# Reordering the down projection of a hybrid decoder layer: pair order, late sums, five low parts by an adding DMA, and Silu one step later

## The chip, the cores and the metric

The kernel runs on one core of one Trainium2 chip. TensorE (PE) multiplies matrices, VectorE (DVE) and ScalarE (ACT) work element by element, GpSimd (POOL) is used little, and SyncE (SP) issues most of the DMAs. Each engine takes its instructions in program order. The metric is the device time of one execution in microseconds (us).

## The reference

One layer on 256 tokens of width 1024, in float32. A normalized input goes through `w_in` into two groups: eight heads of attention (with 256 tokens there is one block, so it is plain causal attention, after QK-norm and rotary), and a gated causal depthwise convolution with layer norm and Silu. Both go through `w_out` and are added to the input. Then comes the feed-forward part, with 2816 inner columns, which the change touches:

```
h = rms_norm(x, norm2_g[l])
x = x + (jax.nn.silu(h @ w_gate[l]) * (h @ w_up[l])) @ w_down[l]
```

## The kernel before, in words

**High and low parts.** To keep float32 accuracy every weight is split into a high part (rounded, type float32r, tile `wh`) and a low part (weight minus high part, tile `wl`). A product is then three matmuls: high by high, low by high and high by low. Weights come from HBM in blocks of 128x2048 (`raw`, a ring of 4, loaded by `load_block` on SP's queue), and are split in pieces of 128x1024, numbered from 0 on. `feed(upto)` converts high parts up to piece `upto + 1` on ACT (L243) and makes low parts up to piece `upto`: on DVE (L207), or, for some pieces, "by DMA": ACT writes the negative of the high part into `wl` (L204) and a DMA on POOL's queue adds the raw piece to it (L205). `wh` and `wl` are rings of 7, so piece j waits until PE has done with piece j-7. A block is reloaded when both its pieces are split.

**Stages.** Pieces 0 to 19 are `w_in`, 20 to 27 `w_out`, 28 to 71 gate and up (each f of 22 has two pieces: eight k tiles of gate and eight of up, for 128 inner columns), from 72 on `w_down`.

**Steps.** The order of the work is written out as steps. `step()` lets each task that is due issue its next part; a task is a generator that yields how many steps it waits. In gate and up there are four steps to an f; `feed` stands ahead of a step and runs 4 pieces ahead of PE (`LEAD`). When an f has reached the middle, its `glu_task` starts: one step later the gate is evicted (`halves`: ACT copies one half of the bank, L273, DVE adds it to the other half, L274), DVE multiplies by the row factor (L786) and ACT takes Silu (L788). Two steps after that the up bank is evicted in the same way and multiplied (L800).

**Plain and Strassen pairs.** The down projection goes over 11 pairs of 256 inner columns. A pair marked P is plain: two pieces, 24 matmuls of 512 columns. A pair marked F is done by a form of Strassen's algorithm with seven products instead of eight (M1, M2, N3, N4, N5, M6, M7, of 3 matmuls each): three pieces, the first of which is a raw quarter pair, the others weight sums made by three DVE adds (`add_up`, L221 to L223), and one extra quarter, `b11`, split apart by `single` (L190 and L191, for product M1). The other operand is sums of activations, `forms` (L810 to L819). All pairs add into the same eight banks of PSUM: M1, N5, M7 and M6 take, in this order, the ring `mm`, which held the gates of f=18 to 21; M2 and N3 take ring `t`; N4 and C22 take ring `s`, which held the ups of f=20 and 21. The last two Strassen pairs end the kernel product by product (`ends`), so that the final sums on DVE and the output DMAs can follow.

`SUMS` tells at which piece of gate and up `add_up` is called ahead of time for the first Strassen pairs; the others are made when the first of their pieces is converted.

Of the kernel before, what the change touches and what calls it, by code (L numbers as in the profile page):

```python
# [21 lines left out]
W = 512  # L22
# [3 lines left out]
NF = FF // P  # L26
# [30 lines left out]
V_PIECE = 21  # L57
SS_WAIT = 3
OUT_LATE = 6
PAIRS = "FPFPFPFPPFF"  # L60
FAST = [p for p in range(NF // 2) if PAIRS[p] == "F"]
PLAIN = [p for p in range(NF // 2) if PAIRS[p] == "P"]
DOWN = 72
DMA_LOW = 40
X_TOK = 12
SUMS = {66: 0, 70: 1}


def _round12(a):
# [59 lines left out]
def build(nc, tc, t):  # L129
    with ExitStack() as ctx:  # L130
        _build(nc, tc, t, ctx)
    keep_order(nc, tc)


def _build(nc, tc, t, ctx):
# [32 lines left out]
    def step():  # L168
        for task in list(tasks):
            while task in tasks and task[0] <= now[0]:  # L170
                try:
                    task[0] = now[0] + next(task[1])
                except StopIteration:
                    tasks.remove(task)
        now[0] += 1
# [4 lines left out]
    def load_block(i, parts=1):  # L180
        if i >= NB:
            return
        r = raw.tile([P, BW], F32, name=f"raw{i}", tag="raw")
        n = BW // parts
        for j in range(parts):
            nc.sync.dma_start(r[:, j * n:(j + 1) * n], t["w"][i - 2][:, j * n:(j + 1) * n])
        blocks[i] = r
# [5 lines left out]
    def new_piece():  # L193
        j = len(pieces)
        pieces.append([wgt.tile([P, PIECE], F32R, name=f"w{s}{j}", tag="w" + s) for s in "hl"])
        i, a = divmod(j * PIECE, BW)
        if j >= DOWN:
            return pieces[-1], down_piece(*down[j - DOWN]), j
        return pieces[-1], blocks[i][:, a:a + PIECE] if i > 1 else None, j

    def low_part(dst, src, by_dma=False):

        if by_dma:
            nc.scalar.activation(dst[1], dst[0].bitcast(F32), AF.Copy, scale=-1.0)  # L204
            nc.gpsimd.dma_start(dst[1].bitcast(F32), src, accum_op=ALU.add)  # L205
        else:
            nc.vector.tensor_tensor(dst[1], src, dst[0].bitcast(F32), op=ALU.subtract)  # L207
# [6 lines left out]
    wsums, b11 = {}, {}  # L214

    def add_up(q):

        if q not in wsums:
            w = blocks[DOWN // 2 + FAST[q]]
            u = wsums[q] = keep.tile([P, 4 * W], F32, name=f"t{q}", tag=("x2T", "big_l")[q % 2])  # L220
            nc.vector.tensor_tensor(u[:, 0:2 * W], w[:, 0:2 * W], w[:, W:3 * W], op=ALU.add)  # L221
            nc.vector.tensor_tensor(u[:, 2 * W:3 * W], u[:, 0:W], w[:, 2 * W:3 * W], op=ALU.add)
            nc.vector.tensor_tensor(u[:, 3 * W:], u[:, 2 * W:3 * W], w[:, 3 * W:], op=ALU.add)  # L223

    def down_piece(p, a):
        w = blocks[DOWN // 2 + p]
        if p in PLAIN:
            return w[:, a * PIECE:(a + 1) * PIECE]
        add_up(FAST.index(p))
        u = wsums[FAST.index(p)]  # L230
        return (w[:, 2 * W:], u[:, 0:2 * W], u[:, 2 * W:])[a]

    def single(q):

        i = DOWN // 2 + FAST[q]
        split(b11[q % 2], blocks[i][:, 0:W], nc.vector)
        load_block(i + RAW)

    def feed(upto):
        last = DOWN + len(down) - 1  # L240
        while len(pieces) <= min(upto + 1, last):
            dst, src, j = new_piece()
            nc.scalar.activation(dst[0], src, AF.Copy)  # L243
            waiting.append((dst, src, j))
        while waiting and waiting[0][2] <= upto:
            dst, src, j = waiting.pop(0)
            low_part(dst, src, DMA_LOW <= j < DOWN and j % 4 == 1)
            if j < DOWN and j % 2:
                load_block(j // 2 + RAW)
            elif j >= DOWN and down[j - DOWN][0] in PLAIN and down[j - DOWN][1]:  # L250
                load_block(DOWN // 2 + down[j - DOWN][0] + RAW)

    def wtile(col, width):
        j, c = divmod(col, PIECE)
        return [p[:, c:c + width] for p in pieces[j]]
# [15 lines left out]
    def halves(out, bank, side):  # L271

        nc.scalar.activation(side, bank[:, T:], AF.Copy)  # L273
        nc.vector.tensor_tensor(out, bank[:, 0:T], side, op=ALU.add)  # L274
# [79 lines left out]
    for kt in range(KT):  # L354
        if kt % 2 == 0:
            dst, _, _ = new_piece()
# [315 lines left out]
    for chunk in range(5):  # L672
        banks = [mm_bank(f"p{chunk}{i}") for i in range(NT)]
        for kt in range(KT):
# [3 lines left out]
            w = wtile(unit * W, W)  # L678
# [104 lines left out]
    def glu_task(f, pg, pu):  # L783
        tg = late.tile([P, T], F32, name=f"tg{f}", tag="tg", bufs=2)
        halves(tg, pg, side(f"gs{f}"))
        nc.vector.tensor_tensor(tg, tg, r_bc, op=ALU.mult)  # L786
        s = late.tile([P, T], F32, name=f"sf{f}", tag="sf", bufs=2)
        nc.scalar.activation(s, tg, AF.Silu)  # L788
        yield max(1, ffn["up"][f] - now[0])
        pair, second = divmod(f, 2)  # L790
        if pair in PLAIN:
            ac = late.tile([P, T], F32, name=f"ac{f}", tag="ac")
        else:
            q = FAST.index(pair)
            if not second:
                pair_sums[q] = late.tile([P, 9 * P], F32, name=f"ps{q}", tag="ps")
            ps = pair_sums[q]
            ac = ps[:, 0:T] if second else ps[:, T:2 * T]
        halves(ac, pu, side(f"us{f}"))
        nc.vector.tensor_tensor(ac, ac, s, op=ALU.mult)  # L800
        if pair in PLAIN:
            a = 2 * PLAIN.index(pair) + second
            nc.scalar.activation(acts[:, 0, a, :], ac, AF.Copy)
            yield 1
            nc.vector.tensor_tensor(acts[:, 1, a, :], ac, acts[:, 0, a, :].bitcast(F32), op=ALU.subtract)
        elif second:


            p3 = ps.rearrange("p (b q) -> p b q", q=P)
            nc.vector.tensor_tensor(p3[:, 4:6], p3[:, 2:4], p3[:, 0:2], op=ALU.subtract)  # L810
            nc.vector.tensor_tensor(p3[:, 6:8], p3[:, 5:6].to_broadcast([P, 2, P]), p3[:, 2:5:2], op=ALU.subtract)
            nc.vector.tensor_tensor(p3[:, 8], p3[:, 2], p3[:, 3], op=ALU.subtract)
            yield 1
            parts = ((forms[q][:, :, 0:3], p3[:, 0:3]), (forms[q][:, :, 3:7], p3[:, 5:9]))
            for to, of in parts:
                nc.scalar.activation(to[:, 0], of, AF.Copy)
            yield 1
            for to, of in parts:
                nc.vector.tensor_tensor(to[:, 1], of, to[:, 0].bitcast(F32), op=ALU.subtract)  # L819
# [16 lines left out]
    for f in range(NF):  # L836
# [6 lines left out]
        a = 0  # L843
        for g, group in enumerate(groups):
            jobs = []
            for z, k in group:
                if a % 4 == 0:
                    if f == a == 0:
                        step()
                    now_at = (off + a * P) // PIECE  # L850
                    if now_at in SUMS and a % 8 == 4:
                        add_up(SUMS[now_at])
                    feed(now_at + LEAD)
# [10 lines left out]
        if f == 0:  # L864
            spawn(glu_task(0, pg, pu), GLU0_WAIT)
            ffn["up"][0] = now[0] + GLU0_WAIT
# [9 lines left out]
    M1, M2, N3, N4, N5, M6, M7, C22 = range(8)  # L876
# [11 lines left out]
    def plain(pair, a):  # L888
        f = 2 * PLAIN.index(pair) + a
        w = pieces[index[pair, a]]  # L890
        for n in range(2):
            step()
            wn = [p[:, n * W:(n + 1) * W] for p in w]
            for l, r in ((0, 0), (1, 0), (0, 1)):
                for i in range(NT):
                    add((M2, N3, N4, C22)[2 * i + n], acts[:, l, f, i * P:(i + 1) * P], wn[r],
                        i == n == r == a == 1 and pair == PLAIN[-1])
# [4 lines left out]
    def seventh(q, m):  # L902
        form, part, side = of[m]
        rhs = b11[q % 2] if part is None else [p[:, side * W:(side + 1) * W] for p in pieces[index[FAST[q], part]]]
        for l, r in ((0, 0), (1, 0), (0, 1)):
            add(m, forms[q][:, l, form, :], rhs[r], r == 1 and q == len(FAST) - 1)

    ends = range(len(FAST) - 2, len(FAST))
    for pair in range(NF // 2 - 2):
        for q in range(1, len(FAST)):  # L910
            if min(FAST[q], FAST[-2]) == pair + 1:
                single(q)
        if pair in PLAIN:
            for a in range(2):
                feed(index[pair, a] + LEAD)
                plain(pair, a)
        else:
            q = FAST.index(pair)
            for part, ms in ((0, (M1, M2, N3)), (1, (N5, M7)), (2, (M6, N4))):
                feed(index[pair, part] + LEAD)  # L920
                step()
                for m in ms:
                    seventh(q, m)
# [12 lines left out]
    m1, u = rest[:, 0, :], rest[:, 1, :]  # L936
# [77 lines left out]
```

## Time and profile before

| | us |
|---|---|
| median of 3 runs | 297.55 (297.11 to 298.29) |
| profiled execution | 300.1 |
| its span, first to last instruction | 298.3 |
| PE busy | 289.8 |
| DVE busy | 245.7 |
| ACT busy | 188.9 |
| POOL busy | 28.2 |

The page shows one execution. It divides the span into 40 slices of 7.46 us and gives each engine's busy share in tenths, and the TensorE clock that was granted (PEclk, 9 for full). A row of the timeline holds the start, the duration, the engine, the line of the kernel, the operation, the tiles (output, then inputs), how many instructions are merged, and in brackets how long the engine had been idle and what released it. A row of the windows holds a stretch of time, its length, and the busy time of each engine in it.

### The profile page before, as it was taken

To read this page: it belongs to the slowest core of one execution; us is meant where nothing else is said; L and a number is where in the kernel's file an instruction comes from. 1 tells how busy PE (TensorE), PEld (TensorE's weight loads), DVE (VectorE), ACT (ScalarE), POOL (GpSimd) and SP (SyncE) were. 2 spreads that over 40 slices of the span, in tenths; PEclk is the share of its full clock that TensorE was granted. 3 is DMA by queue.
4 is the path that set the end of the run, shared out by engine and by line. 5 is a ranking of instruction groups with operands and counts; after the bars stand their busy time and mean duration, and the time that the engine had idled before them with its cause. 6 is when DMAs were issued, how large, how long until landed. Compare 5 with 4: busy or idle time off the path is not lost.

```text
span 298.3 us, 4308 instructions
## 1 busy us (share of the span) xinstructions
PE 289.8 (97%) x1567; PEld 244.6 (82%) x1567; DVE 245.7 (82%) x442; ACT 188.9 (63%) x320; POOL 28.2 (9%) x49
## 2 busy tenths in 40 slices
PE   8999999999999999999999999999999699999994
PEld 6778877678799988898888888888888478888883
DVE  3889995998996998874886785885688899999965
ACT  4777768977638883557767757756645486567400
POOL 0005372000000350001011001101010000000000
PEclk9999999999999999999999999999999959999999
DMA  7999779534313827353767768768756333760003
GB/s 249 418 414 357 301 249 332 193 141 161 123 23 137 341 79 288 124 169 129 226 182 301 233 179 311 249 158 310 262 125 271 141 143 142 281 266 18 0 0 141
DMA packets 11479, 60.92 MB, mean 204 GB/s; under 512 B 1537, under 2 KB 2145, under 8 KB 5570
## 3 DMA queue, kind: packets, MB, share of 16 engines
q1 hardware_dynamic: 9874, 55.14, 49.0%
q0 software_dynamic: 1440, 5.50, 8.6%
q8 instruction: 12, 0.20, 0.3%
q14 instruction: 9, 0.07, 0.1%
q10 hardware_dynamic: 144, 0.00, 0.0%
HBM read 55.40 MB, written 1.05 MB: 189 GB/s over the span
## 4 chain that ended last, share of the span: by engine, by line
PE 73%; DVE 14%; ACT 6%; issue 3%; DMA 2%; DVEq 0%; SPq 0%; ACTq 0%
PE p L685 18%; PE sum L886 16%; PE fg L264 10%; PE fu L264 10%; PE fg L269 5%; PE fu L269 5%; DVE wl L207 4%; ACT wh L243 3%; DMA first<-first 2%; PE po L285 2%; DVE x L932 2%; PE S L519 1%; PE pT L549 1%; DVE g L728 1%; DVE x2T L753 1%
## 5 line engine op out<-in xcount | busy, mean ns | idle before, releaser
L207 DVE TENSOR_TENSOR wl<-raw,wh 128x1024 fp32r<-128x1024 f32 x76 | 92.6, 1233 | 0.3 <-ACT wh L243 0.3
L243 ACT ACTIVATE wh<-raw 128x1024 fp32r<-128x1024 f32 x84 | 86.8, 1048 | 7.6 <-PE sum L886 4.8
L264 PE MATMUL fg<-g,wh 128*128 128x512 f32 x176 | 44.9, 394 | 0.3 <-DVE g L728 0.3
L264 PE MATMUL fu<-g,wh 128*128 128x512 f32 x176 | 44.6, 394 | 0.0
L264 PEld LDWEIGHTS fg<-g,wh 128*128 128x128 f32 x176 | 31.6, 189 | 6.3 <-DVE g L728 0.7
L264 PEld LDWEIGHTS fu<-g,wh 128*128 128x128 f32 x176 | 31.7, 189 | 5.7
L685 PE MATMUL p<-wh,xh 128*128 128x512 f32 x80 | 33.1, 414 | 0.1
L788 ACT ACTIVATE sf<-tg 128x256 f32<-128x256 f32 x22 | 9.2, 418 | 36.7 <-DVE tg L786 36.7
L685 PE MATMUL p<-wh,xl 128*128 128x512 f32 x80 | 31.4, 392 | 0.0
L886 PE MATMUL sum<-wh,forms 128*128 128x512 f32 x72 | 23.2, 405 | 2.7 <-DVE tg L274 2.7
L269 PEld LDWEIGHTS fg<-g,wl 128*128 128x128 f32 x176 | 24.1, 190 | 1.8
L269 PEld LDWEIGHTS fu<-g,wl 128*128 128x128 f32 x176 | 24.1, 190 | 1.7
L685 PE MATMUL p<-wl,xh 128*128 128x512 f32 x80 | 25.2, 395 | 0.0
L269 PE MATMUL fu<-g,wl 128*128 128x256 f32 x176 | 24.8, 282 | 0.0
L269 PE MATMUL fg<-g,wl 128*128 128x256 f32 x176 | 24.8, 282 | 0.0
L886 PE MATMUL sum<-wh,act 128*128 128x512 f32 x80 | 22.7, 408 | 0.0
L886 PEld LDWEIGHTS sum<-wh,act 128*128 128x128 f32 x80 | 16.0, 201 | 3.6
L274 DVE TENSOR_TENSOR tg<-fg,gs 128x256 f32<-128x256 f32 x22 | 9.3, 421 | 11.6 <-ACT gs L273 11.6
L886 PEld LDWEIGHTS sum<-wh,forms 128*128 128x128 f32 x72 | 13.9, 195 | 6.0 <-DVE tg L274 3.2
L243 ACT ACTIVATE wh<-t 128x1024 fp32r<-128x1024 f32 x12 | 12.7, 1057 | 9.7 <-DVE t L221 4.7
L685 PEld LDWEIGHTS p<-wh,xh 128*128 128x128 f32 x80 | 15.2, 190 | 4.2 <-issue 0.7
L685 PEld LDWEIGHTS p<-wl,xh 128*128 128x128 f32 x80 | 15.0, 189 | 3.7 <-DVE wl L207 0.4
(188 smaller groups left out, 491.5 us busy)
## 6 DMA issues: line engine op xcount, KB each, us to landing
raw<-w SPq DMA_DIRECT2D x45, 1024.0 KB, 4.9
wl<-raw POOLq DMA_DIRECT2D x8, 512.0 KB, 4.7
first<-first SPq DMA_DIRECT2D x8, 384.0 KB, 6.8
xtok<-xtok SPq DMA_DIRECT2D x2, 512.0 KB, 9.1
x2T<-xT SPq DMA_DIRECT2D x1, 1024.0 KB, 8.3
out<-x SPq DMA_DIRECT2D x4, 256.0 KB, 2.1
inv<-inv POOLq DMA_DIRECT2D x1, 640.0 KB, 7.0
fwd<-fwd POOLq DMA_DIRECT2D x1, 632.0 KB, 4.8
```

Of the source, the lines that this page charges most:

```text
L207: nc.vector.tensor_tensor(dst[1], src, dst[0].bitcast(F32), op=ALU.subtract)
L243: nc.scalar.activation(dst[0], src, AF.Copy)
L264: nc.tensor.matmul(out.rearrange("p (a q) -> p a q", a=2), w[0], both, start=z in first and z not in seen, stop=False)
L269: nc.tensor.matmul(out[:, 0:T], w[1], both[:, 0, :], start=False, stop=z in last and left[z] == 0)
L274: nc.vector.tensor_tensor(out, bank[:, 0:T], side, op=ALU.add)
L285: nc.tensor.matmul(out, l, r, start=a == 0, stop=a == len(ops) - 1)
L519: nc.tensor.matmul(banks[a][:, out], G["qT"][rows, j, q], G["kT"][rows, j, k], start=True, stop=True)
L549: nc.tensor.transpose(b[:, a * P:(a + 1) * P], p[:, a * P:(a + 1) * P], ident)
L685: nc.tensor.matmul(banks[i], (xh, xh, xl)[a][:, kt, sls[i]], w[a % 2], start=kt == 0 and a == 0, stop=kt == KT - 1 and a == 2 - (order[-1] ...
L788: nc.scalar.activation(s, tg, AF.Silu)
L886: nc.tensor.matmul(banks[m], lhs, rhs, start=first, stop=last)
L932: onto = lambda x, bank, r: nc.vector.scalar_tensor_tensor(x, bank, r, x, op0=ALU.mult, op1=ALU.add)
```

## The change

Six edits, in the code below:

- The order of the pairs: the second and third pairs are plain now; there are still six Strassen and five plain ones.
- `BY_DMA` lists the pieces whose low part is made by DMA: the eight from before (41, 45 to 69) and five of the down projection, 82, 87, 92, 94 and 97. In the new order 82, 87 and 92 are the first pieces of the third, fourth and fifth plain pairs, and 94 and 97 the first pieces of the last two Strassen pairs. The two instructions are issued as soon as the high part is, one piece earlier than before.
- `SUMS` holds only the first Strassen pair. `down_piece` returns the raw part of a Strassen pair without calling `add_up`, so the sums are made when the pair's second piece is converted; for the second Strassen pair that is piece 80, at the first `feed` of the second pair.
- The sums of activations of the last f are made four steps later (`FORMS_LATE`).
- Silu of each f is issued one step after its gate's eviction. The up eviction keeps its step, but for f=0, where it comes one later.
- In part 0 of a Strassen pair M1 stands behind M2 and N3.

```
-PAIRS = "FPFPFPFPPFF"
+PAIRS = "FPPFPFPFPFF"
...
-DMA_LOW = 40
+BY_DMA = [*range(41, DOWN, 4), 82, 87, 92, 94, 97]
 X_TOK = 12
-SUMS = {66: 0, 70: 1}
+SUMS = {66: 0}
+FORMS_LATE = 4
...
         w = blocks[DOWN // 2 + p]
         if p in PLAIN:
             return w[:, a * PIECE:(a + 1) * PIECE]
+        if a == 0:
+            return w[:, 2 * W:]
         add_up(FAST.index(p))
-        u = wsums[FAST.index(p)]
-        return (w[:, 2 * W:], u[:, 0:2 * W], u[:, 2 * W:])[a]
+        return wsums[FAST.index(p)][:, (2 * a - 2) * W:2 * a * W]
...
             nc.scalar.activation(dst[0], src, AF.Copy)
+            if j in BY_DMA:
+                low_part(dst, src, True)
             waiting.append((dst, src, j))
         while waiting and waiting[0][2] <= upto:
             dst, src, j = waiting.pop(0)
-            low_part(dst, src, DMA_LOW <= j < DOWN and j % 4 == 1)
+            if j not in BY_DMA:
+                low_part(dst, src)
...
         s = late.tile([P, T], F32, name=f"sf{f}", tag="sf", bufs=2)
+        yield 1
         nc.scalar.activation(s, tg, AF.Silu)
...
         elif second:
+            if f == NF - 1:
+                yield FORMS_LATE
...
-            for part, ms in ((0, (M1, M2, N3)), (1, (N5, M7)), (2, (M6, N4))):
+            for part, ms in ((0, (M2, N3, M1)), (1, (N5, M7)), (2, (M6, N4))):
```

## The prediction

> **What bounds the kernel now.** I read the page first. Its slices say that TensorE (PE) is busy at 9 tenths or more nearly throughout, with one hole in slice 31 and half the clock in slice 32; the waits of PE then name the hole.
>
> ```profile
> span 298.3 us, 4308 instructions
> PE   8999999999999999999999999999999699999994
> PEclk9999999999999999999999999999999959999999
> PE sum L886 <- DVE tg L274: 2.7, 1, 2.7
> ```
>
> So every other stage is paced by PE itself, and only what closes this hole, or opens a new one, can move the end. The windows round it come next (columns: stretch, its length, busy time of PE, PEld, DVE, ACT, POOL, then granted clock, DMA share, GB/s).
>
> ```profile
> 206.00:232.00 26.00, 26.00 (x152) 22.83 (x150) 20.44 (x35) 15.29 (x28) 1.44 (x2) 1.00 0.65 205
> 217.00:239.20 22.20, 19.44 (x105) 16.25 (x104) 20.19 (x33) 10.25 (x18) 0.86 (x1) 0.98 0.50 166
> 236.05:238.18 2.13, 0.00 (x0) 0.00 (x0) 2.10 (x4) 0.00 (x0) 0.00 (x0) 1.00 0.35 146
> 238.18:245.00 6.82, 6.22 (x15) 4.86 (x16) 6.37 (x11) 5.18 (x9) 0.00 (x0) 0.50 0.43 156
> 245.00:252.00 7.00, 7.00 (x32) 5.78 (x31) 6.88 (x9) 4.14 (x6) 0.00 (x0) 1.00 0.40 151
> 239.20:284.10 44.90, 44.90 (x187) 36.78 (x187) 43.66 (x48) 27.86 (x32) 0.00 (x0) 0.94 0.37 141
> ```
>
> The hole lies where the gate and up projections end and the down projection begins. In it PE does nothing and VectorE (DVE) is never idle; the clock falls to 0.50 at 238.18 and is back at 245.00, so the hole is paid for twice. PE's own rows give the prices.
>
> ```profile
> 228.14 1.12 PE L269 MATMUL fg<-g,wl 128*128 128x256 f32 x8
> 232.07 0.73 PE L886 MATMUL sum<-b11h,forms 128*128 128x512 f32 x2
> 233.13 0.63 PE L886 MATMUL sum<-wh,forms 128*128 128x512 f32 x2
> 235.65 0.39 PE L886 MATMUL sum<-wl,forms 128*128 128x512 f32 x1
> 238.78 1.22 PE L886 MATMUL sum<-wh,forms 128*128 128x512 f32 x2 [2.74 <-DVE tg L274]
> 248.64 0.84 PE L886 MATMUL sum<-b11b,forms 128*128 128x512 f32 x3
> 258.84 0.61 PE L886 MATMUL sum<-b11h,forms 128*128 128x512 f32 x2
> 284.68 0.61 PE L886 MATMUL sum<-b11h,forms 128*128 128x512 f32 x2
> 293.52 0.61 PE L886 MATMUL sum<-wh,forms 128*128 128x512 f32 x2
> ```
>
> Pace: from 258.84 to 284.68 the code issues 21+24+21+24+24 = 114 matmuls (a Strassen pair is 7 products of 3, a plain pair 24): 25.84/114 = 0.2267 us each.
> - Hole, start to start: 238.78 - 235.65 - 0.23 = **2.90**.
> - Half clock: 238.78 to 248.64 holds M6 and N4 of pair 0 and plain pair 1, 30 matmuls. 9.86 - 30 x 0.2267 = **3.06**.
> - At the very start M1 takes 233.13 - 232.07 = 1.06 for three matmuls worth 0.68: **0.38** spent waiting for b11.
>
> What the hole waits for: M6 is the fourth bank of the ring "mm", after M1, N5 and M7, and that bank holds the gate of f=21. Its last matmul is in the row at 228.14, done at 229.26, yet DVE evicts it at 238.31. DVE's queue ahead of that:
>
> ```profile
> 230.61 0.43 DVE L786 TENSOR_TENSOR tg<-tg,r_bc 128x256 f32<-128x256 f32 x1
> 231.07 0.42 ACT L788 ACTIVATE sf<-tg 128x256 f32<-128x256 f32 x1 [2.10 <-DVE tg L786]
> 231.40 0.61 ACT L190 ACTIVATE b11h<-raw 128x512 fp32r<-128x512 f32 x1
> 232.04 0.69 DVE L191 TENSOR_TENSOR b11l<-raw,b11h 128x512 fp32r<-128x512 f32 x1 [1.00 <-ACT b11h L190]
> 233.79 1.22 DVE L221 TENSOR_TENSOR t<-raw 128x1024 f32<-128x1024 f32 x1
> 236.38 0.42 DVE L274 TENSOR_TENSOR ps<-fu,us 128x256 f32<-128x256 f32 x1
> 238.31 0.42 DVE L274 TENSOR_TENSOR tg<-fg,gs 128x256 f32<-128x256 f32 x1
> 241.83 0.42 DVE L274 TENSOR_TENSOR ps<-fu,us 128x256 f32<-128x256 f32 x1
> ```
>
> DVE is late, not PE: the sums of the second Strassen pair sit in DVE's queue from 233.79 to 236.38, ahead of the eviction, and before them DVE waited 1.00 for ScalarE (ACT), which itself had stood 2.10 in front of a Silu.
>
> **The change part by part.**
>
> *The sums (SUMS, down_piece).* add_up of pair 1 leaves step 70: 236.38 - 233.79 = 2.59 of DVE ahead of the eviction goes. With part 0 taken from raw and two plain pairs in front, it is first called when piece 80 is converted, that is by feed(79) at plain pair 1, behind the last gate and up evictions. Piece 79, whose low part then queues behind it, is read only after pairs 0, 1 and 2: 21+24+24 = 69 matmuls, 15.6 us, after 232.07. So it costs nothing on the path as long as DVE keeps that lead.
>
> *Silu one step on.* On ACT the order becomes: gate copy, next step's conversion, Silu. For f=20, single(0) also comes ahead of it, so b11h can go as soon as its copy of the gate is done and DVE's 1.00 before b11l goes. Upstream the same happens at each f:
>
> ```profile
> L788 ACT ACTIVATE sf<-tg 128x256 f32<-128x256 f32 x5 | 2.1, 418 | 8.5 <-DVE tg L786 8.5
> DVE tg L274 <- ACT gs L273: 3.7, 3, 1.7
> L243 ACT ACTIVATE wh<-raw 128x1024 fp32r<-128x1024 f32 x7 | 7.3, 1044 | 0.0
> ```
>
> In 206 to 232 ACT stands 8.5 us before five Silus, and DVE in its turn 3.7 for ACT's gate copies. One conversion of 1.04 put into each such gap brings ACT and DVE nearer to PE. Bounds: nothing upstream, to the 9 us by which the last gate is late. I take only the 1.00 that I can place, and leave the rest as margin. Queued behind the later Silu is the up copy and, on DVE, the product with sf; the up eviction keeps its step (except f=0, one later), and up banks are reused two f later, so 1.04 us of delay has no reader.
>
> *Sum at the hole.* M6's bank is free at 238.73 - 2.59 - 1.00 = 235.14. PE, with no wait at M1, comes to M6 at 232.07 + 15 x 0.2267 = 235.47. Hole 0. Without the 1.00 it would be 0.67, the upper bound. C22, the 29th matmul, is due at 232.07 + 28 x 0.2267 = 238.42 and needs the up bank of f=21, now evicted by 242.25, less 3.59 = 238.66: 0.24 at the worst, nothing if any of the margin comes.
>
> *M1 last in part 0.* b11l (done 232.73) is then wanted six matmuls later, 233.43: the 0.38 goes.
>
> *The clock.* PE now runs without a break past 236.05, so I remove the 3.06 whole. With both bounds above left in (0.67 and 0.24) the clock could still dip; bounds 0 to 3.06.
>
> *Pair order and FORMS_LATE.* Still six Strassen and five plain pairs, so 246 matmuls and the same bytes; 0. Forms of f=21, last in ACT's and DVE's way (L810 to L819), are read only by the last two pairs.
>
> *Five low parts by DMA.* Rows for each operation stand in the trace, since eight such pieces run before 217:
>
> ```profile
> L204 ACT ACTIVATE wl<-wh x8: 1042/1044/1046, 138.4 to 215.7; 128x1024 fp32r<-128x1024 f32 x8
> L205 POOL DMA_DIRECT2D wl<-raw x8: 862/872/928, 139.7 to 217.0; - x8
> DMA to landing us min/median/max: 4.5/4.7/6.5
> L207 DVE TENSOR_TENSOR wl<-raw,wh 128x1024 fp32r<-128x1024 f32 x14 | 16.7, 1219 | 0.3 <-ACT wh L243 0.3
> 251.60 2.35 DVE L207 TENSOR_TENSOR wl<-raw,wh 128x1024 fp32r<-128x1024 f32 x2
> 281.50 2.57 DVE L207 TENSOR_TENSOR wl<-t,wh 128x1024 fp32r<-128x1024 f32 x2
> ```
>
> DVE loses 5 low parts at their back-to-back pace (two in 2.35, one alone 1.22: 1.13 each): 5.7 us. ACT gains 5 x 1.04 = 5.2; it is busy 27.86 of 44.90 in this stage. POOL is idle there (0.00). Cover for DVE: it must have the last low part ready 6.34 us earlier than now. Now it is done at 281.50 + 2.57 = 284.07 and read by M6 of pair 10, the 18th of the closing matmuls, near 284.68 + 17 x 0.2267 = 288.5, so it has 4.4 to spare and must gain at least 1.9. It starts 3.59 earlier, takes 2.59 of sums in and gives 5.7 away: 6.7 gained. Without the DMA parts it would gain 1.0 and the end would be late by about 0.9.
>
> The landing: piece j needs the buffers of j-7. Tightest are 87 and 92: from the end of piece 80 (or 85) to their first reading lie 51 matmuls, 11.56 us (their low part 4 matmuls later still); two ACT passes, the POOL issue and the landing take 2 x 1.04 + 0.87 + 4.7 = 7.7, at the slowest landing seen 9.5. On SP's queue the load of the last raw block now waits until piece 87's DMA has read the block that it replaces: piece 80 ends 84 matmuls after 232.07, at 251.1, plus 7.7 is 258.8, and that load's piece 97 is converted only when piece 90 is done, 174 matmuls in, at 271.5. Nothing on the path. The DMAs up to piece 69 are only issued one piece earlier.
>
> *Total:* 2.90 + 3.06 + 0.38 = 6.34. The profiled execution took 300.1 us (span 298.3 and 1.8 round it); it would become 293.8. The median of the runs, 297.55, is 2.55 below that execution; taking the difference over to it gives **291.2**. Small bounds: with the 0.67 and 0.24 left, 292.1, and with a dip of the clock as well 295.2.
>
> **The rivals.**
>
> *The timed runs have no half clock.* The hole lasts 2.74, and the profiled execution lies 2.55 above the median, close to the 3.06 that the clock costs. If the timed runs never pay it, only 2.90 + 0.38 is won: 294.3. Against it: the three runs agree within 1.2 us, while a gate that catches some executions and not others would spread them by 3; and recording a profile can cost time itself. The Trainium skill ("TensorE: Matmul & The Clock Gate", part 1 and the table of why this matters) asks for no PE-idle gap above about 3 us and lets the clock fall after an idle window of about 3.4; by that a 2.7 us hole would keep full clock and the gain would be the 3.28 of this rival. The trace disagrees for this execution: 0.50 from 238.18 to 245.00.
>
> *The hole shrinks but stays*, because an eviction is still late: 292.1 to 295.2, as above.
>
> *DVE becomes the bound (no change).* It is busy 43.66 of 44.90 from 239.2 to 284.1; if PE only runs into its low parts later, the gain is given back, 297.5. For that DVE would have to finish near 288.5 and not at 284.07 - 6.7 = 277.4, 11 us of unforeseen work or waiting. Against it: five low parts leave, and its idle time comes from ACT.
>
> *Slower: the adding DMA lands late.* Pieces 82, 87 and 92 each stop PE if a landing takes longer than 11.56 + 4 x 0.2267 - 2.95 = 9.5 us. At 12.2 each stop is 2.7, 8.1 in all: 297.55 - 6.34 + 8.1 = 299.3, and 3.06 more for each that halves the clock. It is slower than before from a landing of 11.6 on (three stops of 2.1 outweigh 6.3). Against it: 6.5 is the slowest of eight, and they ran at a DMA share of 0.65 where this stage has 0.37.
>
> **How the numbers follow.** Forecast 0.63; no half clock in the timed runs 0.16; a smaller hole 0.09; DVE the bound 0.07; late DMA 0.05. A measurement here tells 0.5% (1.5 us) from no change. The first three are faster by more than that: 0.88; the fourth is the same: 0.07; the last slower: 0.05. The predicted time is 291.2. The range goes from 290.5 (0.7 below: the fastest run shown lies 0.44 under its median, and the terms are rounded) to 294.6, just past the first rival, and leaves out the last two and part of the third.
>
> **What would show it.** Right: PE's wait on L274 gone; granted clock 1.00 in every slice; the sums of the second Strassen pair on DVE after the gate and up evictions of f=21; Silu's idle before it near nothing; L204 and L205 x13; last matmul near 287.4; span near 292. Wrong: any PE wait above 1 us in the down projection, on wl (DMA), on DVE L207, or on L274 again; or a profiled execution down by 6 with a median down by only 3, which would be the clock rival.

## The result, and the profile after

The changed kernel takes 293.12 us in the median, the kernel before 297.53 in the same comparison: ratio 0.985, 95% interval 0.982 to 0.987. That is 4.4 us faster, inside the range and 1.9 us above the forecast. One of the changed kernel's four runs took 1067.27 us, which nothing on record explains: the ratio leaves it out, and without it the median is 293.07. The profiled execution of the changed kernel is an ordinary one, 293.17 us with a span of 291.4; against the profiled execution of the kernel before the span is 6.9 shorter.

First the page of the changed kernel and PE's waits, of which these are all.

```profile
span 291.4 us, 4317 instructions
PE   8999999999999999999999999999999999999994
PEclk9999999999999999999999999999999999999999
PE warm L335 <- DVE one L318: 1.0, 1, 1.0
PE fg L269 <- DVE g L733: 0.3, 1, 0.3
PE prb L784 <- DVE wide L780: 0.2, 1, 0.2
```

The hole in slice 31 and the half clock in slice 32 are gone, and none of the three small waits that are left lies in the down projection. The timeline at the boundary (lines of the changed kernel stand some 5 to 8 further down):

```profile
228.72 2.00 PE L269 MATMUL fu<-g,wh 128*128 128x512 f32 x8
228.99 0.39 ACT L278 ACTIVATE gs<-fg 128x256 f32<-128x256 f32 x1 [1.28 <-PE fg L274]
229.61 0.42 DVE L279 TENSOR_TENSOR tg<-fg,gs 128x256 f32<-128x256 f32 x1
231.52 0.63 PE L894 MATMUL sum<-wh,forms 128*128 128x512 f32 x2
232.68 0.41 DVE L279 TENSOR_TENSOR ps<-fu,us 128x256 f32<-128x256 f32 x1
234.60 1.22 DVE L222 TENSOR_TENSOR t<-raw 128x1024 f32<-128x1024 f32 x1
234.95 0.62 PE L894 MATMUL sum<-wh,forms 128*128 128x512 f32 x2
287.08 0.39 PE L894 MATMUL sum<-wl,forms 128*128 128x512 f32 x1
```

The gate of f=21 is evicted by 230.03, where before it was 238.73. PE wants its bank (M6) at 234.95, so there are 4.9 us of margin in place of the hole. The sums of the second Strassen pair come behind both evictions, as written. The first and the last of the 246 matmuls start at 231.52 and 287.08, so 245 steps take 55.56 us, 0.2268 each: the pace of before, with no gap.

Of the 6.9 us between the two spans, 6.34 are the three terms of the prediction. The other 0.55 lie before the down projection (it begins at 231.52 instead of 232.07), 0.36 of them before the gate and up stage, where nothing was changed.

But the runs gained 4.4, not 6.9, and the reason for the gain was not the one that the prediction put first. Both came out in the experiments.

### The profile page after: what moved, and what is told of

Read it like the earlier page. It is cut to its first block, busy times and chain, and to the rows that moved or that the text cites. A ratio compares the mean times of both kernels' runs of the same rounds, so it can differ in the third digit from the quotient of the medians.

```text
span 291.4 us, 4317 instructions
## 1 busy us (share of the span) xinstructions
PE 285.8 (98%) x1567; PEld 243.1 (83%) x1567; DVE 240.0 (82%) x437; ACT 198.0 (68%) x325; POOL 32.4 (11%) x54
## 3 DMA queue, kind: packets, MB, share of 16 engines
HBM read 55.40 MB, written 1.05 MB: 194 GB/s over the span
## 4 chain that ended last, share of the span: by engine, by line
PE 86%; DVE 7%; ACT 3%; issue 2%; DVEq 0%
PE p L690 19%; PE sum L894 17%; PE fu L269 13%; PE fg L269 13%; PE fu L274 7%; PE fg L274 7%; DVE wl L208 2%; PE po L290 2%; DVE x L940 2%; PE warm L335 1%; ACT wh L245 1%; PE S L524 1%; PE pT L554 1%; DVE g L733 1%; DVE x2T L758 1%
## 5 line engine op out<-in xcount | busy, mean ns | idle before, releaser
L208 DVE TENSOR_TENSOR wl<-raw,wh 128x1024 fp32r<-128x1024 f32 x71 | 86.9, 1234 | 4.2 <-PE sum L894 2.9
L206 POOL DMA_DIRECT2D wl<-raw x13 | 11.2, 865 | 154.0 <-ACT sf L794 70.9
L894 PE MATMUL sum<-wh,forms 128*128 128x512 f32 x72 | 22.2, 390 | 0.0
L894 PE MATMUL sum<-wh,act 128*128 128x512 f32 x80 | 21.4, 389 | 0.0
L894 PEld LDWEIGHTS sum<-wh,act 128*128 128x128 f32 x80 | 15.0, 188 | 3.1
L690 PEld LDWEIGHTS p<-wh,xl 128*128 128x128 f32 x80 | 15.2, 190 | 2.8
```

The costliest lines, as they stand in the source:

```text
L690: nc.tensor.matmul(banks[i], (xh, xh, xl)[a][:, kt, sls[i]], w[a % 2], start=kt == 0 and a == 0, stop=kt == KT - 1 and a == 2 - (order[-1] ...
L894: nc.tensor.matmul(banks[m], lhs, rhs, start=first, stop=last)
```

## The experiments

Theory A is the prediction's account: the sums in DVE's queue were the main cost, the Silu step a small one. Theory B holds that the Silu step is the change. All ratios are to the kernel before, with 95% intervals.

**One edit alone: Silu one step later.**

```
+        yield 1
         nc.scalar.activation(s, tg, AF.Silu)
```

> The kernel before with one edit: Silu issued one step after the gate's eviction. Theory A (the prediction's sum: Silu is worth the 1.00 us at b11 and little upstream): the bank of M6 comes free at 238.73 - 1.00 = 237.7, PE is there at 235.5, so a hole of 2.3 us stays and the time is 295.5 to 297. Theory B (the later Silu lets ACT and DVE work off the whole backlog during gate and up, as the changed kernel's trace suggests, where the gate of f=21 is evicted 8.7 us earlier, of which the sums are 2.59 and the wait at b11 1.00): the eviction comes near 238.3 - 6.1 = 232.2, no hole, all the gain: 293.2.

Measured: 293.0 us, 0.984 [0.982, 0.986]. This single line gives the whole gain of the change. The waits over the whole span say why; first the kernel before, then this one (engine and line, what it waited for, us in total, times, longest).

```profile
ACT sf L788 <- DVE tg L786: 36.7, 22, 4.8
```

```profile
ACT sf L789 <- DVE tg L786: 9.3, 9, 3.5
ACT us L273 <- PE fu L269: 9.7, 14, 1.0
ACT gs L273 <- PE fg L269: 5.9, 5, 1.5
```

Before, ACT stood 36.7 us in front of Silu, at every one of the 22 f, and never once waited for PE to be done with a gate or an up. With a conversion put into that gap 9.3 are left, and ACT now waits for PE: it has caught up. How late the gate copy comes shows the same: first the kernel before at f=8 and at f=20, then this edit at f=20.

```profile
156.47 2.00 PE L264 MATMUL fu<-g,wh 128*128 128x512 f32 x8
161.66 0.36 ACT L273 ACTIVATE gs<-fg 128x256 f32<-128x256 f32 x1
223.51 2.00 PE L264 MATMUL fu<-g,wh 128*128 128x512 f32 x8
228.61 0.36 ACT L273 ACTIVATE gs<-fg 128x256 f32<-128x256 f32 x1
```

```profile
223.20 2.00 PE L264 MATMUL fu<-g,wh 128*128 128x512 f32 x8
224.39 0.37 ACT L273 ACTIVATE gs<-fg 128x256 f32<-128x256 f32 x1
```

PE is done with a gate when its up begins: at f=20 the copy came 5.1 us later before, and comes 1.2 later now. At f=8 it was as late, 5.2: from f=4 on the copy is between 2.5 and 5.8 us late at every f. So the delay does not grow over the stage; it stands from early on, and the later Silu takes it away. The rest of the change adds nothing to that: 293.0 with this one edit, 293.1 with all six, and PE waits nowhere in the down projection.

**The other edit alone: the sums out of step 70.**

```
-SUMS = {66: 0, 70: 1}
+SUMS = {66: 0}
```

> The kernel before with one edit: SUMS holds only the first Strassen pair, so the second pair's sums are made when its first piece is converted, at the first feed of the down projection. Theory A (the sums in front of the gate's eviction are the main cost, 2.59 us): hole at M6 down to about 0.3 and time 294 to 295. Theory B (the backlog of DVE as a whole counts, and the sums only change places in it): the sums now stand ahead of the up eviction of f=21, which stays at 242.2 while PE wants its bank (C22) at about 238.8: the hole moves to C22, 3.4 us, and the time stays 297 to 298.

Measured: 298.57 us, 1.002 [1.0004, 1.0037]: no gain, a little worse. PE's waits:

```profile
PE sum L886 <- DVE ps L274: 2.4, 1, 2.4
PE sum L886 <- DVE tg L274: 0.2, 1, 0.2
```

The hole at M6 shrank to 0.2, near the 0.3 of the count, and came back 2.4 us long at C22's bank, where the up eviction of f=21 (ps) now stood behind the sums. Here, work moved within the queue of an engine that is behind moved the wait, and did not remove it.

**The change without the Silu step.**

```
-        yield 1
         nc.scalar.activation(s, tg, AF.Silu)
```

> The changed kernel with Silu back at the gate's eviction. Theory A: the bank of M6 comes free at 236.1 against 235.5, C22's at 239.7 against 239.1, together 1.2 us: 293.8 to 294.3. Theory B: the backlog is as it was, less the 2.59 of the sums: the same two short waits of 1.2 in all, and a dip of the clock if they fall into one window, up to 296. Both: slower than the changed kernel, and DVE's gate eviction of f=21 is again 5 us or more later than the 229.6 of the changed kernel.

Measured: 301.44 us, 1.012 [1.010, 1.014]. Both theories were wrong: five of the six edits together make the kernel slower than it was before. The four longest waits of PE behind the start name two things that neither had:

```profile
PE sum L893 <- DMA wl<-raw: 2.5, 2, 1.5
PE sum L893 <- DVE tg L279: 1.5, 1, 1.5
PE fu L269 <- DVE ps L279: 1.2, 1, 1.2
PE fu L269 <- DVE ac L279: 0.4, 1, 0.4
```

PE now waits within gate and up (fu) for banks that DVE has not evicted, so the backlog has grown; and twice for the adding DMA, as in the slower rival. Only in part for its reason, though: the two landed in 5.8 and 8.8 us, under the 9.5 of the rival, and their issue was late too: that of piece 82 came 9.5 us later than in the changed kernel, while PE came to it 5.1 later. These four waits and one of 0.3 come to 5.9 of the 8.3 us by which this run is slower than the changed kernel; the rest is not traced here. The early issue alone, and the run without the five DMA parts, take the two things apart further down.

**The sums put back, in the changed kernel.**

```
-SUMS = {66: 0}
+SUMS = {66: 0, 70: 1}
```

> The changed kernel with the second Strassen pair's sums back at step 70, ahead of the gate's eviction of f=21. Theory A: the eviction is 2.59 us later than planned, a hole of about 2.3 us: 295.4 to 297. Theory B: in the changed kernel the gate of f=21 is evicted by 230.0 and PE wants its bank at 234.9, 4.9 us of margin, so 2.59 cost nothing: 293.1, no hole.

Measured: 292.93 us, 0.983 [0.982, 0.985], no wait of PE in the down projection. As theory B has it: with the Silu step in, the place of the sums is worth nothing.

**Early issue alone.** In the kernel before, the two instructions of a DMA low part are put right behind the high part, one piece earlier; nothing else.

```
             nc.scalar.activation(dst[0], src, AF.Copy)
+            if DMA_LOW <= j < DOWN and j % 4 == 1:
+                low_part(dst, src, True)
             waiting.append((dst, src, j))
...
-            low_part(dst, src, DMA_LOW <= j < DOWN and j % 4 == 1)
+            if not (DMA_LOW <= j < DOWN and j % 4 == 1):
+                low_part(dst, src)
```

> The kernel before with one edit: the eight low parts by DMA are issued right behind their high part, one piece earlier. Theory C (this edit is what makes the changed kernel without the Silu step slower than the kernel before: ACT's negating pass of 1.05 us now stands ahead of an up copy for which DVE waits, so ACT and DVE fall further behind PE): the gate copies of ACT come 6 to 7 us after PE is done with the gate instead of 4 to 5, PE waits for an up bank within gate and up, the hole at M6 grows, 299 to 301. Rival (the pair order or the five DMAs of the down projection cost it, not this): 297.3 to 298.3, as before.

Measured: 301.56 us, 1.011 [1.008, 1.014]: 3.3 us slower from issuing eight passes of ACT, with their DMAs, one piece earlier. PE's waits:

```profile
PE sum L889 <- DVE tg L277: 2.7, 1, 2.7
PE sum L889 <- ACT b11h L190: 1.4, 1, 1.4
PE fu L267 <- DVE ps L277: 1.2, 1, 1.2
PE sum L889 <- DVE ps L277: 0.3, 1, 0.3
PE fu L267 <- DVE ac L277: 0.2, 1, 0.2
```

The hole at M6 stays and 3.1 us of other waits come in front of and behind it. The gate copy of f=20 starts 6.6 us after PE is done with it (5.1 before), that of f=21 6.4 (5.0 before). That ACT's pass of 1.05 us lengthens the round from ACT to DVE and back, because it now stands ahead of an up copy, is the likely reason; what is shown is that this edit alone does it. Theory C holds in that, and in the later gate copies and the wait for an up bank; the hole at M6 did not grow, and the time lies just above its 299 to 301.

**The change without Silu and without the five DMA parts of the down projection.**

```
-        yield 1
...
-BY_DMA = [*range(41, DOWN, 4), 82, 87, 92, 94, 97]
+BY_DMA = [*range(41, DOWN, 4)]
```

> The changed kernel with Silu back at the gate's eviction and without the five DMA low parts of the down projection (the eight from before stay). Theory C: the two waits of PE on the adding DMA (2.5 us) go, DVE has room for the five low parts, the rest stays: 298.5 to 299.5. Rival (DVE is the bound there without them, as the prediction has it): PE waits on L208 instead, 301 or more.

Measured: 300.35 us, 1.007 [1.004, 1.010], between the two expectations. The 2.5 us of waiting for the DMA go, and 1.0 of waiting for DVE's low part comes:

```profile
PE sum L893 <- DVE tg L279: 1.5, 1, 1.5
PE fu L269 <- DVE ps L279: 1.2, 1, 1.2
PE sum L893 <- DVE wl L208: 1.0, 1, 1.0
```

So where DVE runs late, the five DMA parts take a wait of 1.0 off it and bring one of 2.5.

**How much of the Silu step is needed: f=20 and 21 alone, and from f=16 on.** Both are the kernel before with a condition in front of the step.

```
+        if f >= 20:
+            yield 1
```

> The kernel before with Silu one step later for f=20 and 21 alone. By the prediction's term: DVE's 1.00 at b11 and the 0.38 at M1 go, a hole of about 2.3 at M6 stays, 296 to 297. Theory B (what counts is the backlog worked off over many f) says the same for these two alone. Rival (the last two Silus are what matters): no hole, 293.1.

Measured: 296.71 us, 0.994 [0.992, 0.996]. PE's wait at M6 is 2.2 us where the count from 1.00 at b11 gave 2.3. The prediction's term for the Silu step was right for the two f that it looked at.

```
+        if f >= 16:
+            yield 1
```

> The kernel before with Silu one step later from f=16 on. Theory B: each Silu takes 0.95 to 1.7 us of idle time out of ACT, six of them more than the 4 us by which the gate copy of f=16 is late, so ACT is back at PE by the end of gate and up: no hole, 293.1 (up to 294 if the last 1 us is missing). Rival (the lag has to be worked off from the first f on): a hole of 1 us or more, 294.5 to 296.

Measured: 293.78 us, 0.985 [0.982, 0.988], with 0.3 us of waiting at M6. Six f win back nearly all: the gate copy, 4.15 us late at f=16, is 1.55 late at f=21. The standing delay is worked off over several f: with two the hole is 2.2, with six 0.3, with all of them 0.

**The price of a hole and of the clock.** The changed kernel, with n additions on DVE whose result is not used, ahead of the gate eviction of f=21.

```
+        if f == NF - 1:
+            junk = keep.tile([P, 4 * W], F32, name="junk", tag="big_l")
+            for _ in range(n):
+                nc.vector.tensor_tensor(junk[:, 0:2 * W], wsums[0][:, 0:2 * W], wsums[0][:, 0:2 * W], op=ALU.add)
```

With n = 3:

> The changed kernel with three more 128x1024 additions on DVE (1.14 us each, 3.4 in all, their result unused) ahead of the gate eviction of f=21. The margin there is 4.9 us, so nothing is to be seen: 293.1, no wait of PE.

Measured: 295.53 us, 0.991 [0.989, 0.993], 2.4 us above what was expected. M6 does not wait, as counted, but two other places do:

```profile
PE sum L898 <- DMA wl<-raw: 2.3, 2, 1.7
253.37 0.73 PE L898 MATMUL sum<-wl,act 128*128 128x512 f32 x2 [0.68 <-DMA wl<-raw]
265.52 0.74 PE L898 MATMUL sum<-wl,act 128*128 128x512 f32 x2 [1.66 <-DMA wl<-raw]
```

These are the low parts of pieces 82 and 87; they landed in 5.9 and 9.5 us. So the margin of the adding DMAs is smaller than 3.4 us. In the changed kernel itself it can be read for piece 87: the issue on POOL's queue, its landing in us (the last column), the first matmuls of that piece that read the low part, a window behind the issue, and the DMA queues from 255 to 258 (packets, MB, share of the 16 engines; q1 holds the loads of raw blocks, q0 the adding DMA).

```profile
253.01 0.85 POOL L206 DMA_DIRECT2D wl<-raw  x1 [8.08 <-ACT wl L205]
wl<-raw POOLq DMA_DIRECT2D x1, 512.0 KB, 8.2
263.05 0.61 PE L894 MATMUL sum<-wl,act 128*128 128x512 f32 x2
252.00:254.00 2.00, 2.00 (x11) 1.65 (x10) 0.88 (x2) 1.66 (x2) 0.85 (x1) 1.00 1.05 442
q1 hardware_dynamic: 87, 0.62, 74.2%
q0 software_dynamic: 29, 0.12, 19.8%
```

It lands at 253.0 + 8.2 = 261.2 and is read at 263.05: 1.8 us to spare. The DMA engines are full just then (share 1.05), where the stage's mean before was 0.37, and until 258 most of them serve the loads: two raw blocks of 1 MB were issued about 3.0 and 1.5 us ahead of it. Piece 82, with one such load ahead of it, lands in 5.8 and has 3.0 to spare. The Trainium skill has a rule for this in "DMA: Bandwidth & Descriptors" (section "Issuing engines are not separate DMA queues"): DMAs run on the same 16 engines and interleave, whichever engine issued them. The two queue rows agree.

With n = 7:

> The changed kernel with seven such additions, 8.0 us in all: a hole of 3.1 us at M6 is put back by itself. Without any fall of the clock PE then also waits 0.6 for C22's bank: 296.7. With half the clock for one window of 3.4 us, 1.7 more, of which that 0.6 is hidden: 297.8. For two windows, as in the profiled execution of the kernel before: 299.2. If the clock falls only after an idle window of 3.4 us, it stays full in all runs: 296.7.

Measured: 300.57 us, 1.008 [1.006, 1.009], more than any of the three cases, since the adding DMA wait, unknown when this was written, comes on top. PE's waits are 3.7 at M6, 0.6 more than counted, and 1.6 for the DMA; the profile has one stretch of half clock, from 239.9 to 243.3. With these 297.8 becomes 300.0. The clock was below full in every execution, its mean over the span 0.991 or 0.992; as the hole was longer than 3.4, this run cannot tell whether a shorter one would do.

The clock itself is best seen in the run with Silu later for f=20 and 21, whose hole is 2.2 us. Twelve executions: five at full clock, median 295.8, seven with a mean of 0.994, median 297.0. Windows of one microsecond of one of the seven:

```profile
237.00:238.00 1.00, 1.00 (x5) 0.83 (x6) 1.00 (x2) 0.69 (x2) 0.00 (x0) 1.00 0.00 0
238.00:239.00 1.00, 1.00 (x4) 0.77 (x3) 1.00 (x2) 1.00 (x3) 0.00 (x0) 0.51 0.00 0
241.00:242.00 1.00, 1.00 (x4) 0.79 (x4) 1.00 (x3) 0.51 (x1) 0.00 (x0) 0.78 0.97 410
```

Half clock from 238.0 to 241.4, one stretch of 3.4 us; the profiled execution of the kernel before had two such, 6.8. The fall does not come at a fixed time of idleness: here it came 1.1 us after the hole had ended, in the kernel before 2.1 us into it, and the profiled execution of the early-issue run kept full clock behind a hole of 2.7. The executions of the kernel before that ran beside the experiments show three groups: full clock 13 (median 297.3), one stretch 36 (298.2), two 3 (299.5). So one stretch costs 0.9 net, two 2.2, although PE loses about 1.7 in one (half of 3.4, an estimate) and 3.06 in the two of the profile. Part can lie in the hole, as 0.6 us of the stretch in the kernel before did; the rest would be given back behind it. I take this to be the wait for C22's bank, which a slower PE reaches later. Two runs point that way, and neither settles it. The early-issue run, profiled at full clock, waits 0.3 there behind the same hole (`ps` in its waits above), and the kernel before, at half clock, does not; but 0.8 is to be explained. In the run with the sums alone the hole is at C22 itself, so nothing is left to be given back behind it: eleven executions with one stretch have the median 298.6, the single one at full clock took 296.5, 2.1 less.

**What is left of the change without Silu, the five DMA parts and the early issue.** Pair order, later sums, FORMS_LATE and M1 last.

```
-        yield 1
...
-BY_DMA = [*range(41, DOWN, 4), 82, 87, 92, 94, 97]
+BY_DMA = [*range(41, DOWN, 4)]
...
-            if j in BY_DMA:
-                low_part(dst, src, True)
...
-            if j not in BY_DMA:
-                low_part(dst, src)
+            low_part(dst, src, j in BY_DMA)
```

> The changed kernel with Silu back, without the five DMA parts, and with the eight DMA parts issued at their old place: what is left of the change is the pair order, the later sums, FORMS_LATE and M1 last. By the prediction's sum (2.59 us of sums out of DVE's queue): M6's bank is free at 236.1 and wanted at 235.5, C22's at 239.7 and wanted at 239.3, the 0.38 at M1 is gone: about 1.2 us above the changed kernel, 294.3, and no fall of the clock. Rival (the sums only change places in the backlog, as when they were moved alone): 297 or more, with PE waiting for C22's bank.

Measured: 296.89 us, 0.996 [0.994, 0.997]; here too the truth lies between.

```profile
PE sum L890 <- DVE wl L208: 0.9, 1, 0.9
PE sum L890 <- DVE tg L276: 0.6, 1, 0.6
PE sum L890 <- DVE ps L276: 0.3, 1, 0.3
283.60 2.06 DVE L936 SCALAR_TENSOR_TENSOR x<-sum,rstd,x 128x512 f32<-128x512 f32 x3
```

The two holes are 0.6 and 0.3, the expected 0.67 and 0.24 almost to the digit, so the sums' move with the new pair order does shorten the hole. What the expectation left out is the end: PE waits 0.9 for a low part of DVE, and DVE then begins its final sums at 283.60 without a pause, behind PE. The prediction gave the same 0.9 for a kernel without the DMA parts but with the later Silu, which is another case; that the two agree is chance.

**The n = 3 run again, without the five DMA parts.**

```
-BY_DMA = [*range(41, DOWN, 4), 82, 87, 92, 94, 97]
+BY_DMA = [*range(41, DOWN, 4)]
```

> The changed kernel with three more additions on DVE ahead of the gate eviction of f=21 (3.4 us), and without the five DMA parts of the down projection. Theory D (in the run with the five DMA parts it was the adding DMAs, landing in 8 us and more beside the raw loads, that had no margin, not DVE): 293.1, PE waits for nothing. Rival (DVE has no margin for 3.4 us): PE waits on DVE L208 near the end, 294.5 or more.

Measured: 294.32 us, 0.987 [0.986, 0.989]. PE waits for nothing in the down projection, so the 2.3 us of the n = 3 run were the DMAs' own, and theory D is right about PE. It is not 293.1 all the same: DVE makes its last low part so late that the final sums follow on it at once (first row; second row: the changed kernel, where the same sums wait for PE).

```profile
280.80 2.06 DVE L944 SCALAR_TENSOR_TENSOR x<-sum,rstd,x 128x512 f32<-128x512 f32 x3
```

```profile
280.71 1.41 DVE L940 SCALAR_TENSOR_TENSOR x<-sum,rstd,x 128x512 f32<-128x512 f32 x2 [1.97 <-PE sum L894]
```

DVE's last sum starts and ends 0.75 us later than in the changed kernel, although PE is done 0.3 earlier. So DVE's margin at the end is also used up by 3.4 us once the five low parts are back on it.

## Why the prediction was right, and where it was not

**The bound.** Right: the hole and what follows from it was what there was to win in the down projection. After the change PE runs it without a gap, and the span came out at 291.4 against 292.0.

**The sum at the hole.** The size was right, the attribution wrong. The step that failed is "I take only the 1.00 that I can place, and leave the rest as margin". The rest was the gain: the Silu step alone evicts the gate in time, and the 2.59 of the sums, which the prediction put first, are worth nothing once it is in and nothing alone. They are worth something only with the new pair order and without the Silu step: holes of 0.6 and 0.3 are left then, and the run is 1.3 us faster than the kernel before. The rows were there: 8.5 us of ACT's idle time in front of five Silus, and a gate copy that is 2.5 to 5.8 us late at every f from f=4 on, long before the sums come. The prediction counted what stood in the queues at the boundary only.

**M1 last.** The 0.38 went, but it goes with the Silu step alone too (no wait for b11 is left in that run), so this edit did not earn it.

**The clock.** The term of 3.06 is mis-sized for the timed runs, and the step that failed is "taking the difference over to it": a gain that holds for one execution was taken off a median of others. The profiled execution had two stretches of half clock, which 3 of 52 later ones had; most have one, at 0.9 net. With 0.9 in its place the sum is 2.90 + 0.9 + 0.38 = 4.2, against 4.4 measured, but that agreement is partly luck. The comparison's own runs of the kernel before took 297.11, 297.51, 297.55 and 298.29; the first three are shorter than any of the 36 with one stretch (297.62 and more), so by their times they probably ran at full clock. The rival of the timed runs at full clock was nearer (294.3), but not right either: only a quarter of the 52 ran so, and between executions at full clock the gain is 297.3 - 293.1 = 4.2, not its 3.28. The 0.9 that it lacks stays open; a wait for C22's bank at full clock, as above, would be part of it. The difference of 2.55 between the profiled execution and the median was no cost of profiling, since the changed kernel's profiled execution is as long as its runs; the second stretch explains 1.3 of it and the first 0.9. The Trainium skill ("TensorE: Matmul & The Clock Gate", part 1) lets the clock fall after an idle window of about 3.4 us that runs freely, and its table of why this matters warns of gaps above about 3. The stretches of 3.4 agree with such a window. The threshold does not: holes of 2.2 and 2.7 us lowered the clock in most executions.

**Early issue.** "The DMAs up to piece 69 are only issued one piece earlier" was priced at nothing. Alone it costs 3.3 us, and that term, put at nothing, is a second step that failed. The Silu step covers it; of the edits that were run by themselves it is the most expensive without that cover.

**The five DMA parts.** Right in that PE never waits for them in the changed kernel. Wrong in "the end would be late by about 0.9" without them: in the run without the five and with 3.4 us of extra work on DVE, PE still waits for nothing, and the run with the Silu step alone has no DMA part in the down projection and is as fast. A wait of 0.9 to 1.0 for DVE's low part comes only where the Silu step is missing. And the margin of piece 87 was 1.8 us, not the 3.9 of the count (11.56 - 7.7), because the landing was taken from a stage where the last raw load was issued 4 us or more ahead of the DMA: 8.2 us in place of 4.7. The slower rival had 0.05; the run without Silu shows 2.5 us of such waits, to which late issues added.

**Pair order and FORMS_LATE.** Nothing on the path is to be seen of them, as costed; no run has either by itself.

## What to carry to other kernels

When an in-order engine reaches a boundary late, look at whether it was already late through the stage before, not only at what stands in its queue at the end: a wait of 1.7 us at every tile (36.7 over 22), filled with work that was due anyway, was worth more here than moving a job of 2.59 out of the way. An instruction moved earlier on such an engine need not be free; here it cost 3.3 us, likely because it delayed what the other engine waited for behind it. And a DMA's landing time holds for the traffic that it was measured in.

## What the runs showed of the hardware

- A hole of 2.2 us of PE lowered the granted clock in 7 of 12 executions, one of 2.4 (the sums alone) in 11 of 12, one of 2.7 (the kernel before) in 39 of 52, one of 3.7 in 5 of 5; the length of each hole is read from one profile. The clock was half for 3.4 us, or twice that. The net cost of one stretch was 0.9 to 1.2 us, and 2.1 in the run with the sums alone, against its single execution at full clock.
- An adding DMA of 512 KB landed in 4.5 to 6.5 us in the gate and up stage of the kernel before. In the down projection of the changed kernel four of the five landed in 4.5 to 5.8, and the one issued behind two loads of 1 MB in 8.2.
